# RWKV scans: the pairwise products of two heads on the two row halves of TensorE's array

## The chip, the core and the metric

The kernel runs on one of the eight cores of a Trainium2 chip. A core has five engines that run side by side, each with its own queue of instructions: TensorE (PE, matrix products; PEld are its weight loads), VectorE (DVE), ScalarE (ACT), GpSimd (POOL) and SyncE (SP, which here issues most DMAs). They work on SBUF, 128 partitions of on-chip memory; TensorE writes its results to PSUM, eight banks of 2 KB in each partition. A matmul multiplies a stationary operand (the weights, up to 128 rows by 128 columns) with a moving operand of up to 512 columns; the rows are what is summed over.

The metric is the time of one execution on the device in microseconds. The kernel before took 1816.26 us, the median of three runs (1816.13 to 1817.83).

## The reference

One layer of a hybrid encoder for 1024 tokens of width 1024, in float32: a normalized input is projected, the columns go to a windowed attention, to a bidirectional RWKV-7 mixer and to gates; an MLP with squared ReLU and a gated embedding follow. What the change touches is the RWKV mixer, a recurrence over the tokens, once forward and once backward, for 8 heads of 64:

```python
def rwkv7_bidir_scan(r, w, k, v, a, b):
    ...
    def step(state, inp):
        r_t, w_t, k_t, v_t, a_t, b_t = inp
        sa = jnp.einsum('dbhij,dbhj->dbhi', state, a_t)
        state = (state * w_t[..., None, :] + sa[..., :, None] * b_t[..., None, :]
                 + v_t[..., :, None] * k_t[..., None, :])
        y = jnp.einsum('dbhij,dbhj->dbhi', state, r_t)
        return state, y
```

## The kernel before

The recurrence is computed in chunks of 64 tokens: 16 chunks, two directions. The program takes them as 16 steps `s`; in each, direction `d=0` works on chunk `s` and `d=1` on chunk `15 - s`. Inside a chunk the recurrence becomes matrix products. For each head the scaled vectors of the chunk lie in DRAM as `ra_d` (the 64 columns of `a`, then the 64 of `r`) and `bk_d` (`b` and `k`), heads in four pairs: the 64 channels of a pair's even head on partitions 0 to 63, those of the odd head on partitions 64 to 127. `own` (line 692) names these halves.

**The products.** `products(s, d)` (line 1027) forms, for each head, all products of `b` and `k` with `a` and `r`: a block of 128 x 128 per head, summed over the 64 channels. A pair's two heads share the partitions, so before the change the moving operand `rms[d]` is a tile with two blocks of columns per pair: block 0 has the even head's rows, block 1 the odd head's, and the other rows are zeros, written once by two memsets on GpSimd (lines 790 to 792). One matmul of 128 rows by 256 columns then gives both heads. Two pairs fill one PSUM bank; VectorE multiplies the bank with a triangular mask and writes four heads of `gm`. Then `load_products` (line 795) asks SP for the operands of the next step.

**PSUM.** `ps_gps` (line 1024) takes a bank from a ring of two, tag `gps`. The ring is shared: the products (`gps`), the transposes of `operands` (`tmps`, line 1057), the blocks of `low_products` (`lps`, line 720), the quarter blocks of `inverse_off` (`qps`) and the sums of `epilogue` (`mups`). A bank can be written again when its reader is done.

**The rest of a step.** `wa_part` and `wb_part` sum `wps`; it is copied to `Wt` (lines 1086 and 1087), half on VectorE and half on ScalarE. `u_part` multiplies with the inverse `zi` into `ups`, copied to `UV` (lines 1095 and 1096). `s_part` (`sps`) makes the next state, `y_part` (`yps`) the output. Many of these are matmuls on 64 columns that alternate between the two column halves of the array. `load_step` (line 1040) loads the other operands, `operands` transposes `bkc` into `tm` and scales `rac`.

**The inverse.** Every four steps, `low_products` forms small blocks (`lps`, matmuls on quadrants of 64 x 64), `inverse` (line 734) inverts the 32 x 32 triangles of the next four steps on VectorE, with 62 elementwise instructions between transposes (`Lp`, `Z`, `Zn`, `Zt`), and `inverse_off` completes them on TensorE.

**The order.** Scan matmuls are issued through `mmo`, which keeps them in program order on TensorE. Between them `fill(n)` issues `n` matmuls of independent work (the generator `beside`: the gates' projection, `gmm`, then the attention's output, `uaps`), so that TensorE has something to do while other engines copy. The instructions of the other engines are put in order by the framework's scheduler before the kernel runs; each engine then works its queue in that order. A step `s` runs: products of step s+2, d=0; load_step; 5 fills; `lps` if s is 1, 5 or 9; 4 fills; `u_part`; 3 fills; products of step s+2, d=1; 4 fills; `lps` if s is 0, 4 or 8; `s_part`, `y_part`, `wa_part`; 5 fills; `operands`; 7 fills; at s = 3, 7, 11 the inverse's end; `wb_part`. Ahead of the loop stand the products of steps 0 and 1.

Of the kernel before, what the change touches and what calls it, by code (L numbers as in the profile page):

```python
# [9 lines left out]
F32 = mybir.dt.float32  # L10
F32R = mybir.dt.float32r
AF = mybir.ActivationFunctionType
ALU = mybir.AluOpType
# [4 lines left out]
P = 128  # L18
# [6 lines left out]
NP = 4  # L25
# [112 lines left out]
def block_kernel(ctx: ExitStack, tc: tile.TileContext, I: dict, out: bass.AP):  # L138
    nc = tc.nc

    def pool(stack, name, bufs=1, **kw):
        return stack.enter_context(tc.tile_pool(name=name, bufs=bufs, reuse_waits="tile", **kw))
# [4 lines left out]
    def const(name, shape):  # L147
        t_ = G.tile(shape, F32, name=name)
        nc.sync.dma_start(t_, I[name])
        return t_  # L150

    ra_d = DR.tile([ND, NCH, P, NP, P], F32, name="ra_d")
# [53 lines left out]
    def mmo(*a, **kw):  # L206

        tc.keep_in_program_order(nc.tensor.matmul(*a, **kw))  # L208
# [86 lines left out]
    with ExitStack() as s0:  # L295
# [98 lines left out]
        for t in range(NT):  # L394
# [8 lines left out]
            h, tq = divmod(t, 4)  # L403
            tsl = slice(tq * P, (tq + 1) * P)
            qkv = QW.tile([P, 768], F32, name="qkv", bufs=2)
            pss = [PT0.tile([P, 384], F32, name="psq", bufs=4) for _ in range(2)]
# [30 lines left out]
        for h in range(2):  # L437
            ps = PMM.tile([P, 512], F32, name="mm", tag="mm", bufs=2)
# [13 lines left out]
        for h in range(2):  # L452
            ps = PT0.tile([P, 512], F32, name="z13", tag="psq", bufs=4)
# [10 lines left out]
    gmask = const("gmask", [P, ND, P])  # L464
# [226 lines left out]
    NB = 4  # L691
    own = [slice(0, 64), slice(64, 128)]
    oth = [slice(64, 128), slice(0, 64)]

    def chunk(s, d):
        return s if d == 0 else NCH - 1 - s
# [90 lines left out]
    BP = pool(sB, "prod")  # L787
    zi = zi_tile(BI, "zi")

    rms = [BP.tile([P, 2, NP, P], F32, name=f"rm{i}") for i in range(2)]  # L790
    for t_ in rms:
        nc.gpsimd.memset(t_, 0.0)
    prods = {}

    def load_products(s, d):

        c = chunk(s, d)
        for q in range(2):
            nc.sync.dma_start(rms[d][own[q], q], ra_d[d, c][own[q]])
        b_ = BP.tile([P, NP, P], F32, name="bkp", bufs=2)  # L800
        nc.sync.dma_start(b_, bk_d[d, c])
        prods[s, d] = b_

    lts, zzs, lows = {}, {}, {}
    with ExitStack() as s2:
# [16 lines left out]
        for n in range(NT):  # L822
# [6 lines left out]
            for kv in range(2):  # L829
# [6 lines left out]
                for h in range(4):  # L836
                    sc = PA.tile([P, nk * P], F32, name="sc", tag="sc", bufs=2)
                    for j in range(2):
                        nc.tensor.matmul(sc, qT[:, 4 * kv + h, :], kT[:, kv, j, k0 * P:k1 * P], start=(j == 0), stop=(j == 1))
                    nc.vector.tensor_tensor_reduce(  # L840
                        out=sm[:, h, 0:nk * P], in0=sc, in1=band[:, b0:b0 + nk, :].rearrange("p b t -> p (b t)"), scale=1.0,
# [30 lines left out]
            if n == LOW_AT:  # L872
                lts[0] = list(low0)[-1]
                for d in range(ND):
                    load_products(0, d)
# [140 lines left out]
    gm = [AC[0].tile([P, NB, NH, P], F32, name=f"gm{d}", tag=f"ab{d}", bufs=1) for d in range(ND)]  # L1016
# [7 lines left out]
    def ps_gps(shape, name):  # L1024
        return PB.tile(shape, F32, name=name, tag="gps", bufs=2)

    def products(s, d):

        b_ = prods.pop((s, d))
        for h in range(2):  # L1030
            ps = ps_gps([P, 2, 2, P], "gps")
            for j in range(2):
                mmo(ps[:, j], b_[:, 2 * h + j, :], rms[d][:, :, 2 * h + j, :], start=True, stop=True)
            nc.vector.tensor_tensor(  # L1034
                out=gm[d][:, s % NB, 4 * h:4 * h + 4, :], in0=ps.rearrange("p j q t -> p (j q) t"),
                in1=gmask[:, d, :].unsqueeze(1).broadcast_to([P, 4, P]), op=ALU.mult)
        if s + 1 < NCH:
            load_products(s + 1, d)

# [106 lines left out]
    for d in range(ND):  # L1146
        products(0, d)
        fill(FILL0)
# [4 lines left out]
    def second_step():  # L1153
        fill(FILLQ)
        wps.append(wa_part(0))
        for d in range(ND):
            products(1, d)
            fill(FILL0)
# [5 lines left out]
    for s in range(NCH):  # L1164
# [21 lines left out]
        if more:  # L1186
            products(s + 2, 0)
# [150 lines left out]
    with ExitStack() as s7:  # L1338
# [16 lines left out]
        for i in (4, 5, 6, 7, 0, 1, 2, 3):  # L1355
            t = torder[i]
# [39 lines left out]
        for i in range(NT):  # L1396
# [6 lines left out]
            t = torder[i]  # L1403
# [282 lines left out]
    for ip, (lr_, rr_, bs, fresh) in enumerate(PRODS):  # L1686
        if fresh:
            banks[bs] = [acc() for _ in range(4)]
        for p in range(NPR):
# [5 lines left out]
            for i in range(4):  # L1695
                isl = slice(i * P, (i + 1) * P)
                for j, (x_, y_) in enumerate(((sh, th_), (sh, tl_), (sl, th_))):
                    nc.tensor.matmul(banks[bs][i], x_[:, isl], y_, start=fresh and p + j == 0,  # L1698
                                     stop=p == NPR - 1 and j == 2, skip_group_check=True)
# [8 lines left out]
            if ip == 0 and 0 <= p - (NPR - T1EARLY - NPRE) < NPRE:  # L1708
                q = p - (NPR - T1EARLY - NPRE)
# [3 lines left out]
            if ip == 1 and p % 2 == 0:  # L1713
                e, i = divmod(p // 2, 4)
                t = torder[4 * e + i]
# [11 lines left out]
        for i in range(4):  # L1727
            b_ = banks[bs][i]
# [87 lines left out]
```

## Time and profile before

| what | us |
|---|---|
| median of three runs | 1816.26 |
| profiled execution | 1818.63 |
| its span, first to last instruction | 1816.9 |
| the scan, from the first product to the last `yps` | 521.9 to about 884 |
| granted TensorE clock, mean over the span | 0.977 |

The profile is of one execution. A row of the timeline gives start, length, engine, line, operation, the tile written and the tiles read, and in brackets the idle time of the engine before it with what ended it. Matmuls are pipelined: the next one starts before the one before has ended, so lengths of single matmuls add up to more than the busy time, and the distance of starts is the rate. A float32 matmul leaves two records, one for each of its passes. `L208` is the helper `mmo`, so such rows are told apart by their tiles. A row of the view by stretches gives, for each engine, its busy time and its instructions in the stretch, then the granted clock.

### The profile page before, as it was taken

The numbers are of one execution on the slowest core, as the hardware profiler recorded it, in microseconds if no ns is written. First come the engines' busy times: TensorE is split into PE (matmuls) and PEld (weight loads), VectorE is DVE, ScalarE is ACT, GpSimd is POOL, SyncE is SP. The second block draws the span as 40 slices with busy tenths as digits, with TensorE's granted clock in tenths as the row PEclk, the third lists the DMA queues.
The fourth block names the chain that finished last, engine by engine and source line by source line (L and its number), as shares of the span: only waits on it lengthen the run. The fifth ranks groups of instructions, "written<-read, shape, count | busy, mean of one in ns | idle before, by whom it ended". The sixth has DMA issues, their size and how long they took to land. (4 is left out here: it accounts for less than half of the span.)

```text
span 1816.9 us, 29645 instructions
## 1 busy us (share of the span) xinstructions
PE 1714.2 (94%) x11288; PEld 1376.5 (76%) x11288; DVE 1135.8 (63%) x1931; ACT 883.1 (49%) x1624; POOL 321.7 (18%) x265
## 2 busy tenths in 40 slices
PE   7999888989999898988889989999999999999998
PEld 7977666766677777776667867888888888888887
DVE  5646777745845646575564277766766887685442
ACT  5546666547764555455542154544444444454221
POOL 3454544532132112112142000000000000000000
PEclk9999999999999999989999989999999999999999
DMA  5462344674377474576576214444456984574111
GB/s 198 99 183 81 117 145 145 197 202 115 98 201 203 141 196 148 158 199 197 175 225 198 93 47 151 151 152 161 143 163 214 324 262 122 187 221 135 62 41 47
DMA packets 281998, 285.96 MB, mean 157 GB/s; under 512 B 49408, under 2 KB 195712, under 8 KB 281728
## 3 DMA queue, kind: packets, MB, share of 16 engines
q1 hardware_dynamic: 273600, 270.76, 48.3%
q0 software_dynamic: 7824, 12.59, 2.5%
q8 instruction: 89, 1.46, 0.3%
q10 hardware_dynamic: 432, 0.73, 0.1%
q14 instruction: 53, 0.43, 0.1%
HBM read 203.26 MB, written 80.74 MB: 156 GB/s over the span
## 5 line engine op out<-in xcount | busy, mean ns | idle before, releaser
L188 POOL TENSOR_TENSOR wlo<-wst,whi 128x512 fp32r<-128x512 f32 x100 | 149.6, 1508 | 313.1 <-ACT whi L187 262.4
L1698 PE MATMUL ff2ps<-tl,sh 128*128 128x512 f32 x448 | 174.4, 389 | 0.1
L1698 PE MATMUL ff2ps<-th,sl 128*128 128x512 f32 x448 | 174.3, 389 | 0.0
L1698 PE MATMUL ff2ps<-th,sh 128*128 128x512 f32 x448 | 173.9, 389 | 0.0
L175 POOL TENSOR_TENSOR rstd<-ms,neghalf 128x1 f32<-128x1 f32 x24 | 13.3, 554 | 792.9 <-DVE ms L173 792.9
L187 ACT CAST sh<-sst 128x512 fp32r<-128x512 f32 x109 | 67.8, 622 | 99.5 <-PE ff2ps L1698 50.3
L188 DVE TENSOR_TENSOR sl<-sst,sh 128x512 fp32r<-128x512 f32 x109 | 75.1, 689 | 47.4 <-ACT sh L187 47.2
L1698 PEld LDWEIGHTS ff2ps<-tl,sh 128*128 128x128 f32 x448 | 84.1, 188 | 18.2 <-DVE tl L188 0.5
L1698 PEld LDWEIGHTS ff2ps<-th,sh 128*128 128x128 f32 x448 | 84.0, 188 | 17.7 <-ACT th L187 0.3
L1698 PEld LDWEIGHTS ff2ps<-th,sl 128*128 128x128 f32 x448 | 84.1, 188 | 17.5
L187 ACT CAST whi<-wst 128x512 fp32r<-128x512 f32 x100 | 60.7, 619 | 47.5 <-DMA wst<-in_w_in_dram 16.1
L187 ACT CAST w1h<-w1st 128x512 fp32r<-128x512 f32 x48 | 28.5, 621 | 101.1 <-DMA w1st<-in_w_ff_dram 64.1
L188 DVE TENSOR_TENSOR w1l<-w1st,w1h 128x512 fp32r<-128x512 f32 x48 | 31.9, 688 | 52.2 <-ACT w1h L187 52.2
L208 PE MATMUL gps<-rm,bkp 128*128 128x256 f32 x256 | 62.4, 386 | 1.3 <-ACT tm L1061 0.8
L1034 DVE TENSOR_TENSOR gm<-gps,gmask 128x512 f32<-128x512 f32 x64 | 43.7, 685 | 29.5 <-PE gps L208 29.5
L218 PE MATMUL gmm<-hh,wlo 128*128 128x512 f32 x144 | 59.3, 412 | 0.0
L214 PE MATMUL gmm<-hh,whi 128*128 128x512 f32 x144 | 59.2, 411 | 0.0
L216 PE MATMUL gmm<-hl,whi 128*128 128x512 f32 x144 | 59.2, 411 | 0.0
L1086 DVE COPY Wt<-wps 64x512 f32<-64x512 f32 x16 | 10.9, 680 | 71.3 <-PE wps L208 71.3
L208 PEld LDWEIGHTS gps<-rm,bkp 128*128 128x128 f32 x256 | 47.2, 189 | 10.9 <-issue 1.4
L226 PE MATMUL mm<-hh,whi 128*128 128x512 f32 x128 | 51.5, 402 | 3.3 <-ACT z L520 3.3
L188 DVE TENSOR_TENSOR w1l<-ssum,w1h 128x512 fp32r<-128x512 f32 x64 | 43.0, 688 | 16.9 <-ACT w1h L187 16.9
(409 smaller groups left out, 5056.8 us busy)
## 6 DMA issues: line engine op xcount, KB each, us to landing
wst<-in_w_in_dram SPq DMA_DIRECT2D x92, 256.0 KB, 3.5
tst<-in_w_ff_dram SPq DMA_DIRECT2D x80, 256.0 KB, 4.0
w1st<-in_w_ff_dram SPq DMA_DIRECT2D x32, 512.0 KB, 5.2
hid_S<-h SPq DMA_DIRECT2D x64, 256.0 KB, 2.1
sst<-hid_S SPq DMA_DIRECT2D x64, 256.0 KB, 2.8
hid_A<-h SPq DMA_DIRECT2D x48, 256.0 KB, 2.0
sst<-hid_A SPq DMA_DIRECT2D x45, 256.0 KB, 3.9
ra_d<-ra SPq DMA_DIRECT2D x8, 1024.0 KB, 4.5
```

The lines of the kernel that those rows point to most:

```text
L175: nc.gpsimd.tensor_tensor(out=r, in0=ms, in1=neghalf.broadcast_to([P, width]), op=ALU.pow)
L187: a = nc.scalar.copy(hi, src)
L188: b = (lo_eng or nc.vector).tensor_tensor(out=lo, in0=src, in1=hi.bitcast(F32), op=ALU.subtract)
L208: tc.keep_in_program_order(nc.tensor.matmul(*a, **kw))
L214: mm(ps, ah, bh, start=(i == 0), stop=False)
L216: mm(ps, ah, bl, start=False, stop=False)
L218: mm(ps, al, bh, start=False, stop=(i == n - 1))
L226: nc.tensor.matmul(ps, ah, bh, start=(i == 0), stop=False)
L1034: nc.vector.tensor_tensor(out=gm[d][:, s % NB, 4 * h:4 * h + 4, :], in0=ps.rearrange("p j q t -> p (j q) t"), in1=gmask[:, d, :].unsqueeze ...
L1086: nc.vector.tensor_copy(Wt[own[0], 0], wp[own[0]])
L1698: nc.tensor.matmul(banks[bs][i], x_[:, isl], y_, start=fresh and p + j == 0, stop=p == NPR - 1 and j == 2, skip_group_check=True)
```

## The change

The zeros go, and with them the memsets. `rms[d]` holds the pair's rows once, as they lie in DRAM, loaded by one DMA instead of two. Each pair's product becomes two matmuls of 64 rows by 128 columns: the even head on partitions 0 to 63, the odd head on 64 to 127, each with its own rows of the weights. All even heads of a direction go to one bank, all odd heads to the other; the mask is applied to each bank, and the four heads go to every second place of `gm`.

```diff
-    rms = [BP.tile([P, 2, NP, P], F32, name=f"rm{i}") for i in range(2)]
-    for t_ in rms:
-        nc.gpsimd.memset(t_, 0.0)
+    rms = [BP.tile([P, NP, P], F32, name=f"rm{i}") for i in range(2)]
     prods = {}
 
     def load_products(s, d):
 
         c = chunk(s, d)
-        for q in range(2):
-            nc.sync.dma_start(rms[d][own[q], q], ra_d[d, c][own[q]])
+        nc.sync.dma_start(rms[d], ra_d[d, c])
         b_ = BP.tile([P, NP, P], F32, name="bkp", bufs=2)
         nc.sync.dma_start(b_, bk_d[d, c])
         prods[s, d] = b_
...
     def products(s, d):
 
         b_ = prods.pop((s, d))
-        for h in range(2):
-            ps = ps_gps([P, 2, 2, P], "gps")
-            for j in range(2):
-                mmo(ps[:, j], b_[:, 2 * h + j, :], rms[d][:, :, 2 * h + j, :], start=True, stop=True)
+
+        pss = [ps_gps([P, NP, P], "gps") for _ in range(2)]
+        for j in range(NP):
+            for q in range(2):
+                mmo(pss[q][:, j], b_[own[q], j, :], rms[d][own[q], j, :], start=True, stop=True)
+        for q in range(2):
             nc.vector.tensor_tensor(
-                out=gm[d][:, s % NB, 4 * h:4 * h + 4, :], in0=ps.rearrange("p j q t -> p (j q) t"),
-                in1=gmask[:, d, :].unsqueeze(1).broadcast_to([P, 4, P]), op=ALU.mult)
+                out=gm[d][:, s % NB, q::2, :], in0=pss[q],
+                in1=gmask[:, d, :].unsqueeze(1).broadcast_to([P, NP, P]), op=ALU.mult)
         if s + 1 < NCH:
             load_products(s + 1, d)
```

## The prediction

> **What bounds the kernel now.** I read the page first: how busy each engine is over the whole span, and the row of the products that the change rewrites.
>
> ```profile
> span 1816.9 us, 29645 instructions
> PE 1714.2 (94%) x11288; PEld 1376.5 (76%) x11288; DVE 1135.8 (63%) x1931; ACT 883.1 (49%) x1624; POOL 321.7 (18%) x265
> ...
> L208 PE MATMUL gps<-rm,bkp 128*128 128x256 f32 x256 | 62.4, 386 | 1.3 <-ACT tm L1061 0.8
> ```
>
> TensorE (PE) is busy 94% of the span, and the 32 calls of `products` hold it for 62.4 us: 256 records, since each of the 128 float32 matmuls leaves two, one for each of its passes. So the first guess is that shorter products shorten the run. An average over stages can mislead, so I cut the scan into stretches and read each one.
>
> ```profile
> core 0: us, PE busy (x) PEld busy (x) DVE busy (x) ACT busy (x) POOL busy (x), PEclk, DMA share, GB/s
> 545.00:573.80 28.80, 28.31 (x390) 22.61 (x388) 8.88 (x13) 12.78 (x24) 4.46 (x5) 1.00 0.70 189
> 573.80:616.20 42.40, 36.06 (x460) 29.60 (x458) 40.39 (x83) 18.43 (x41) 10.14 (x11) 0.99 0.66 190
> ...
> 758.00:801.50 43.50, 36.16 (x528) 29.58 (x523) 42.02 (x101) 19.22 (x42) 7.36 (x9) 0.98 0.74 207
> 801.50:850.00 48.50, 45.55 (x648) 37.50 (x650) 22.24 (x33) 30.69 (x55) 8.96 (x8) 0.84 0.63 180
> ```
>
> The scan takes 16 steps, and every fourth one starts an `inverse` on VectorE (DVE). From 545.0 to 573.8 PE is busy 28.31 of 28.80 us and DVE 8.88: PE is the limit. From 573.8 to 616.2 it is turned round: DVE 40.39 of 42.40 us, PE 36.06. The view of waits says whether DVE waits for anything there, and the timeline how the stretch ends.
>
> ```profile
> DVE tmp L749 <- POOL Z L744: 0.2, 1, 0.2
> DVE gm L1034 <- PE gps L208: 0.2, 1, 0.2
> ```
>
> ```profile
> 613.76 1.85 DVE L756 STREAM_TRANSPOSE Zt<-Z 128x1024 f32<-128x1024 f32 x1
> 615.49 0.65 DVE L1095 COPY UV<-ups 64x512 f32<-64x512 f32 x1
> 616.07 1.25 DVE L1034 TENSOR_TENSOR gm<-gps,gmask 128x512 f32<-128x512 f32 x2
> ```
>
> ```profile
> 616.19 1.98 PE L208 MATMUL sps<-UV,tm 128*64 128x64 f32 x32 [4.04 <-DVE UV L1095]
> ```
>
> In 42.4 us DVE waits 0.4 us, and at the end PE stands still for 4.04 us until DVE, done with the inverse, copies `UV`. **Whatever PE saves inside such a stretch only lengthens that wait.** There are three (the third is 758.0 to 801.5: DVE 42.02 of 43.50 us), and in each lie five calls of `products`: d=1 of step 4k+1 and both of steps 4k+2 and 4k+3. That is 15 of the 32.
>
> **The change part by part.** *The matmuls.* A call now issues 4 matmuls of 128 rows by 256 columns, half of them zeros; then 8 of 64 rows by 128 columns, alternating between the array's two row halves. The trace has no 64x128 tile. Its nearest rows, first a stretch cut out around one burst of `lps` (length, then busy time and records of PE, PEld and ACT), then the timeline:
>
> ```profile
> 553.50:554.30 0.80, 0.69 (x32) 0.56 (x32) 0.00 (x0) 1.00 0.34 74
> ```
>
> ```profile
> 563.51 1.09 PE L208 MATMUL wps<-Sb,rac 128*64 128x128 f32 x16
> 564.54 1.99 PE L208 MATMUL gps<-rm,bkp 128*128 128x256 f32 x8
> ...
> 567.30 0.39 PE L208 MATMUL gmm<-hl,whi 128*128 128x512 f32 x1
> 567.62 0.27 PE L208 MATMUL lps<-la,lb 64*64 64x64 f32 x1
> ```
>
> ```profile
> 564.66 0.68 DVE L1086 COPY Wt<-wps 64x512 f32<-64x512 f32 x1 [6.93 <-PE wps L208]
> ```
>
> The first row is a burst of `lps`, quadrants of 64x64: 32 records in 0.69 us. They use both row halves, write two banks, and run on one another's heels, four abreast. The second is `wps`: 16 records that stream 128 columns, on alternating column halves, in 1.09 us, two abreast. The new product is also 16 records of 128 columns. A product now takes 1.99 us here and 1.89 on the step shown below, so a pass of 256 columns is (1.89 - 0.38)/7 = 0.216 us (0.38 being the own length of a record: the page's 386 ns) and one of 128 columns 0.108. If row halves overlap as column halves and quadrants do, its length is about that of `wps`, 1.09 us. If not, 16 passes of half the present length take what 8 whole ones do, 1.9 us. I take overlap, since `lps` shows both row halves at work at once.
>
> *The edges.* The array is now entered and left in another tile shape.
>
> ```profile
> 636.48 0.40 PE L208 MATMUL gmm<-hl,whi 128*128 128x512 f32 x1
> 636.81 1.15 PE L208 MATMUL ups<-Wt,zi 128*64 128x64 f32 x32
> 637.89 0.50 PE L208 MATMUL gmm<-hh,wlo 128*128 128x512 f32 x1
> 638.22 0.40 PE L208 MATMUL gmm<-hh,whi 128*128 128x512 f32 x1
> 638.46 0.40 PE L208 MATMUL gmm<-hl,whi 128*128 128x512 f32 x1
> 638.69 1.89 PE L208 MATMUL gps<-rm,bkp 128*128 128x256 f32 x8
> 640.23 0.58 PE L208 MATMUL gmm<-hh,wlo 128*128 128x512 f32 x1
> 640.65 0.39 PE L208 MATMUL gmm<-hh,whi 128*128 128x512 f32 x1
> ...
> 641.11 0.40 PE L208 MATMUL gmm<-hh,wlo 128*128 128x512 f32 x1
> 641.44 0.27 PE L208 MATMUL lps<-la,lb 64*64 64x64 f32 x1
> ```
>
> Into `ups`, a tiled shape, it takes 636.81 - 636.48 = 0.33 us; into `gps` of the full shape 638.69 - 638.46 = 0.23. The new shape costs 0.10 us more to enter. From the start of `ups` to the second `gmm` behind it are 638.22 - 636.81 = 1.41 us; `ups` streams 16 x 64 columns two abreast, the new product 8 x 128, as many. From the start of `gps` to the second `gmm` are 640.65 - 638.69 = 1.96 us. **A product behind `gmm` (d=1) gives back 1.96 - 1.41 - 0.10 = 0.45 us.** Behind `wps` (d=0) the array is in a tiled shape already and the product lasts 0.10 longer: 2.06 - 1.41 = **0.65 us**. All 32: 16 x 1.10 = 17.6 us.
>
> [...]
>
> *The evictions.* Both copies to `gm` now wait for all eight matmuls, since each bank gets its last block at the end, and both banks of the ring `gps` (two, shared with `lps`, `tmps`, `qps`) are held from the start. The order on DVE stays.
>
> ```profile
> 639.75 0.69 DVE L1034 TENSOR_TENSOR gm<-gps,gmask 128x512 f32<-128x512 f32 x1 [1.01 <-PE gps L208]
> 640.62 0.69 DVE L1034 TENSOR_TENSOR gm<-gps,gmask 128x512 f32<-128x512 f32 x1 [0.17 <-PE gps L208]
> ```
>
> ```profile
> 641.44 0.13 PEld L208 LDWEIGHTS lps<-la,lb 64*64 64x64 f32 x1 [0.37 <-DVE gm L1034]
> ```
>
> Now the copies end at 1.75 and 2.62 us after the product's start, and `lps`, 2.75 after it, goes 0.13 us behind the second. Then: the last pair starts at about 0.85 (seven waves of 0.108 and 0.1 for the edge). The second copy now starts 640.62 - (638.69 + 1.89 - 0.38) = 0.42 us behind the start of the last pass, 0.31 with a pass half as long: 1.16. Two copies back to back take 1.25 (the row at 616.07): 2.41; plus the 0.13, with rounding: **`lps` cannot start before 2.53 us, though PE would be there at 1.41 + 2 x 0.23 + 0.33 = 2.2**. So the d=1 product of steps 4k gives back only 2.75 - 2.53 - 0.10 = 0.12 us, and d=0 of steps 4k+1, which `lps` also follows (567.62 - 564.54 = 3.08), 3.08 - 2.53 = 0.55; `Wt` ahead of it on DVE ends at 565.34, before either copy. The strided target costs nothing by the equal count of elements; 0.1 us a copy would be 0.1 us at each such wait, 1 us in all.
>
> *The start.* Four calls, 521.9 to 541, each with four `gmm` and then the ring: 0.12 us apiece. Behind the first two PE stands still anyway:
>
> ```profile
> 535.85 0.63 PE L208 MATMUL wps<-UV,gm 128*64 128x64 f32 x14 [1.35 <-issue]
> ```
>
> I count two, 0.24 us. **Sum on PE:** start 0.24; steps 0 and 1, whose first product follows `gmm`, 0.45 + 0.12 + 0.55 = 1.12; steps 4, 5 and 8, 9, 2 x (0.65 + 0.12 + 0.55) = 2.64; steps 12 and 13, with no inverse and no `lps`, 2 x 1.10 = 2.20. Together **6.2 us** of the 17.6; bounds 0 and 17.6.
>
> *The memsets and the transfers.* `rms` loses its zeros, and with them two memsets.
>
> ```profile
> 375.47 1.86 POOL L792 MEMSET rm<- 128x1024 f32 x2
> 377.27 1.13 POOL L824 DMA_DIRECT2D qT<-qT_d  x2
> ```
>
> ```profile
> 384.06 0.71 PE L839 MATMUL sc<-kT,qT 128*128 128x256 f32 x4 [2.03 <-DMA qT<-qT_d]
> ```
>
> They stand ahead of the issue of `qT` on POOL, and PE then waits 2.03 us for `qT`. Without them the issue comes 1.86 us sooner. Bounds: 0, if the landing is set by the other transfers, and 1.86; I take **1.5 us**, near the upper, since the wait is longer than the memsets. On SP a load issues two DMAs for three, of the same bytes; SP is not what PE waits for in the stretches above, so nothing.
>
> *The clock.* The long wait at 616 has an aftermath.
>
> ```profile
> 616.19:618.86 2.67, 2.67 (x50) 2.67 (x52) 1.71 (x3) 2.60 (x3) 0.00 (x0) 0.50 0.00 0
> 618.86:622.00 3.14, 3.14 (x87) 2.98 (x84) 1.23 (x3) 1.34 (x4) 1.04 (x2) 1.00 0.41 121
> ```
>
> Behind the 4.04 us PE ran 2.67 us at half clock: 1.3 us lost on its path. From 801.5 to 850.0, behind the third inverse, the granted clock is 0.84: 0.16 x 48.5 = 7.8 us lost. The two calls of step 4k+3 lie before that wait and make it about 1.1 us longer, so I add **1.0 us** (bounds -1.3 and +5).
>
> Forecast: -6.2 - 1.5 + 1.0 = **-6.7 us**. The profiled execution, span and what lies around it, took 1818.63 us and would take 1811.9; it lay 2.4 above the median of the runs shown, 1816.26, so the median goes to **1809.6 us**.
>
> **The rivals.**
>
> *All of it counts* (17.6 + 1.9): 1797 us. It asks that DVE's order change so that `UV` no longer stands behind the inverse. For: PE's 94%. Against: the 4.04 us, and 0.4 us of DVE waits.
>
> *The clock takes it.* The gate closes behind more waits, or for longer: +5 in place of +1, 1813.6 us; with the memsets' 1.5 us hidden too, 1815. For: 0.84 behind the third inverse. Against: the stretch that PE fills, 545.0 to 573.8, has 1.00. [...]
>
> *The halves do not overlap*, the other side: row halves that stream 128 columns into all 128 partitions of two banks take turns. Then a product is 8 x 0.108 = 0.86 us longer than forecast: d=0 costs 0.21 more than now, d=1 0.41, and at the ring 0.31 and 0.74. Two calls at the start 1.5, steps 0 to 9 (0.41 + 0.74 + 0.31) + 2 x (0.21 + 0.74 + 0.31) = 4.0, the last two steps 1.2: +6.7, less 1.5, plus 1: 1822.5 us. It decides as soon as a pair's second half starts 0.1 us behind the first, instead of on its heels. Against it speaks `lps`. It is also the case where the change does not do what it says.
>
> **How the numbers follow.** Forecast 0.60 (its own range 1805 to 1812.5), clock 0.20, all of it 0.08, no overlap 0.07; 0.05 for an order of the engines that comes out otherwise, to either side. I leave out "all of it", "no overlap" and the tails: 1802 to 1817. About 0.2%, 3.6 us, is what a measurement of this kernel tells from no change: faster below 1812.6, slower above 1819.9. Faster: nearly all of the forecast, "all of it" and half of the rest, 0.68; same: the clock and the edge of the forecast, 0.22; slower: no overlap and the other tails, 0.10.
>
> **What would show it.** A burst of 16 `gps` records near 1.1 us, not 1.9. `lps` behind d=1 waiting for `gm` some 0.3 us. The wait of `sps` for `UV` near 616 longer than 4.04 us, the stretch still about 42 us. The wait for `qT` well under 2.03 us. Wrong I would be if DVE idled in that stretch, if the half-clock time beyond 600 us grew by more than 10 us, or if the ring held PE elsewhere too.

## The result and the profile after

The kernel after takes 1829.9 us, the median of nine runs (1821.07 to 1837.85), against 1818.22 for the kernel before (nine runs, 1816.13 to 1822.27): a ratio of 1.0053, with a 95% interval of 1.0035 to 1.0070. It is slower; the forecast was 1809.6 us. 0.001 of the ratio is 1.8 us here.

The profiled execution took 1830.82 us. From its page, the head and the costliest group of ACT, and then the view of the cores, first of after, then of before:

```profile
span 1829.0 us, 30110 instructions
PE 1714.9 (94%) x11544; PEld 1371.7 (75%) x11544; DVE 1137.5 (62%) x1931; ACT 883.1 (48%) x1624; POOL 317.5 (17%) x263
...
L1066 ACT ACTIVATE rac<-rac,Dt 128x128 f32<-128x128 f32 x120 | 39.2, 394 | 44.5 <-DMA rac<-ra_d 44.5
```

```profile
core 0: 1829.0 us, clock 0.968
```

```profile
core 0: 1816.9 us, clock 0.977
```

PE is busy as long as before (1714.2) although its work is shorter. An estimate from these rows: the clock missing from full speed was 0.023 x 1816.9 = 42 us and is 0.032 x 1829.0 = 59, so 17 us more were lost to half clock. PE's idle time was 1816.9 - 1714.2 = 102.7 and is 114.1, 11 us more. The span grew by 12, so the work itself, at full clock, fell by about 16 us. That is near the 17.6 counted for all 32 products. The saving was made, then given back twice: as waits and as half clock. (These are two single executions. Over all nine of after the mean clock is 0.970, over the 31 of before in the first comparison below 0.977: some 13 us.)

Which waits are new? The view of waits on PE, three rows of after:

```profile
PE tmps L1058 <- ACT lt L729: 7.1, 2, 3.7
PE qps L208 <- DVE Zn L755: 5.9, 1, 5.9
PE tmps L1058 <- ACT lv L983: 4.8, 1, 4.8
```

The first is not among before's at all; the other two were 4.5 and 2.5. Step 4 shows how the first arises. The timelines of PE and of ACT, after:

```profile
651.52 1.97 PE L1058 MATMUL tmps<-ident,bkc 128*128 128x128 f32 x8 [3.42 <-ACT lt L729]
```

```profile
650.81 0.40 ACT L1066 ACTIVATE rac<-rac,Dt 128x128 f32<-128x128 f32 x1 [6.08 <-DMA rac<-ra_d]
651.12 0.63 ACT L729 COPY lt<-lps 128x256 f32<-128x256 f32 x2
```

and ACT in the same step of before:

```profile
647.58 0.65 ACT L729 COPY lt<-lps 128x256 f32<-128x256 f32 x2 [1.81 <-PE lps L208]
651.39 0.69 ACT L1067 ACTIVATE rac<-rac,Dt 128x128 f32<-128x128 f32 x2 [3.16 <-DMA rac<-ra_d]
```

Line 1066 scales `rac`, an operand of step 6. In after its first piece stands **ahead** of the two `lt` copies in ACT's queue. ACT keeps to that order: it stands idle for 6.08 us until the transfer of `rac` lands, while the `lps` banks lie full behind it (the last of their matmuls started at 647.22 us, the first copy at 651.12); `tmps` needs one of these banks, and PE waits 3.42 us. In before the copies ran first, and the scaling waited behind them. Over the whole span ACT idles 44.5 us ahead of these scalings, in before 23.6. No line of the diff names `lt`, or the scaling. The order is the scheduler's, and it made another one for the changed program.

### The profile page after: what moved, and what is told of

It reads as the page before. It is cut to its first block, busy times and chain, and to the rows that moved or that the text cites. A ratio compares the mean times of both kernels' runs of the same rounds, so it can differ in the third digit from the quotient of the medians.

```text
span 1829.0 us, 30110 instructions
## 1 busy us (share of the span) xinstructions
PE 1714.9 (94%) x11544; PEld 1371.7 (75%) x11544; DVE 1137.5 (62%) x1931; ACT 883.1 (48%) x1624; POOL 317.5 (17%) x263
## 5 line engine op out<-in xcount | busy, mean ns | idle before, releaser
L1066 ACT ACTIVATE rac<-rac,Dt 128x128 f32<-128x128 f32 x120 | 39.2, 394 | 44.5 <-DMA rac<-ra_d 44.5
L752 DVE TENSOR_TENSOR Z<-Z,tmp 128x31 f32<-128x31 f32 (+15 forms) x124 | 50.2, 405 | 2.4
```

Of the source, the lines that this page charges most:

```text
L752: nc.vector.tensor_tensor(out=Z[:, t + 1:32, 0:m], in0=Z[:, t + 1:32, 0:m], in1=tv, op=ALU.add)
L1066: nc.scalar.activation(out=r_, in_=r_, func=AF.Copy, scale=Dt[:, d, j, s - 1:s])
```

## The experiments

`after(x, y)` is a helper of the kernel: it tells the scheduler to put x behind y on the same engine. Here it moves instructions of ACT; nothing computed changes. All kernels were timed in five rounds beside the kernel before, in four comparisons, each on another chip: e1 to e4, e5 to e8, e9 to e11, and e12 with e13. Where two experiments are compared, their ratios to before are subtracted and the half-widths of the intervals added as squares.

| kernel | median us | ratio to before, 95% interval |
|---|---|---|
| after | 1829.9 | 1.0053 (1.0035 to 1.0070) |
| e1 `lt` first | 1819.99 | 1.0010 (0.9994 to 1.0025) |
| e2 two loads | 1812.55 | 0.9971 (0.9952 to 0.9991) |
| e3 matmuls only | 1818.57 | 1.0002 (0.9984 to 1.0019) |
| e4 no overlap | 1827.99 | 1.0049 (1.0026 to 1.0072) |
| e5 after's order in before | 1820.20 | 1.0014 (0.9997 to 1.0031) |
| e6 `lt` and `pT` pins | 1828.18 | 1.0038 (1.0021 to 1.0056) |
| e7 two loads, `tm` first | 1802.92 | 0.9903 (0.9886 to 0.9921) |
| e8 one load, `tm` and `pT` pins | 1813.68 | 0.9971 (0.9955 to 0.9988) |
| e9 after, `tm` first | 1810.35 | 0.9958 (0.9942 to 0.9974) |
| e10 before, `tm` first | 1809.53 | 0.9959 (0.9944 to 0.9973) |
| e11 one load in the scan, `tm` first | 1805.20 | 0.9938 (0.9918 to 0.9958) |
| e12 e7 without overlap | 1803.51 | 0.9912 (0.9878 to 0.9947) |
| e13 matmuls only, `tm` first | 1802.93 | 0.9901 (0.9878 to 0.9924) |

**The order or the change itself?** e1 moves one scaling behind the `lt` copies, in after:

```diff
-                    nc.scalar.activation(out=r_, in_=r_, func=AF.Copy, scale=Dt[:, d, j, s - 1:s])
+                    a = nc.scalar.activation(out=r_, in_=r_, func=AF.Copy, scale=Dt[:, d, j, s - 1:s])
+                    if s in (6, 10):
+                        after(a, last_lt[-1])
```

> The changed kernel with one thing put back: at steps 4 and 8 ScalarE copies `lt` before it scales the `rac` of two steps later, which wait for their transfer. Theory A, order: the new order of the queues costs the time, and of its 12.1 us (profiled span 1829.0 against 1816.9) this place costs about 3.5 us at each of two steps, wait and clock; so 1821 to 1824 us, and the waits of tmps for lt (3.7 us at 740, 3.4 at 648) are gone. Theory B, the products themselves (both banks held, eviction late, the clock closing behind longer waits): within 2 us of the changed kernel, 1828 to 1832.

e2 takes back the single load and keeps the rest:

```diff
-        nc.sync.dma_start(rms[d], ra_d[d, c])
+        for q in range(2):
+            nc.sync.dma_start(rms[d][own[q]], ra_d[d, c][own[q]])
```

> The changed kernel with the operand still loaded by two DMAs of one half each, as before; everything else as changed. In its ScalarE queue `lt` stands ahead of `rac` again at steps 4 and 8. Theory A: the order came from the DMA that is saved, so 1810 to 1819 us, with the product's gain showing. Theory B: 1826 to 1832, as the same matmuls, banks and evictions run.

e3 puts only the new matmuls and banks into before, with the zeros, the memsets and the two loads:

```diff
-                mmo(ps[:, j], b_[:, 2 * h + j, :], rms[d][:, :, 2 * h + j, :], start=True, stop=True)
+                mmo(pss[q][:, j], b_[own[q], j, :], rms[d][own[q], q, j, :], start=True, stop=True)
```

> The kernel before with the new matmuls and banks alone: the zeros, the memsets and the two loads stay. Its ScalarE queue also has `lt` first. Theory A: 1811 to 1818 us (the forecast's 6.2 us of TensorE time less 1 for the clock, without the 1.5 us of the memsets; somewhat more if the queues come out otherwise). Theory B: 1825 or more.

e4 is after with neighbouring matmuls on the same rows:

```diff
-        for j in range(NP):
-            for q in range(2):
+        for q in range(2):
+            for j in range(NP):
```

> The changed kernel with the eight matmuls in the other order: the four even heads first, then the four odd heads, so that neighbours use the same rows and cannot overlap. A burst of the products should last about 16 x 0.108 + 0.27 = 2.0 us against 1.17. Its ScalarE queue has `lt` first at steps 4 and 8. If the overlap is worth on the path what the forecast said, it lies 8 to 13 us above the variant with two loads; if TensorE's time in the products does not matter at all, within 3 us of it.

e1 and e3 came out some 1 us outside their ranges, e2 inside its own, and e4 15 us above e2, where 8 to 13 were expected. e1 wins back 0.43% of after's time with no other difference than ACT's order (and a few issues on SP and POOL); the `tmps` waits for `lt` are gone from its trace. e2 wins back 0.82% (half-width 0.27) and is faster than before. So neither the matmuls nor the banks made after slow. e3 shows that this is not the whole story: without the new load and without losing the memsets, the new matmuls alone gain nothing. e4 is level with after and 0.78% (half-width 0.30) behind e2. That looked like the price of the overlap; but e4 has one load and another order than both (its ACT runs the `lt` copies first, as before did), so it was taken up again in e12, at one order.

**How much of it is the order?** Four more, in one comparison. e5 gives before the order of after at the one place, e6 adds to e1 a pin in the attention part, where `po` of after waits for a `pT` copy behind a weight cast:

```profile
395.94 0.62 ACT L187 CAST whi<-wst 128x512 fp32r<-128x512 f32 x1 [2.77 <-DMA wst<-in_w_in_dram]
396.47 0.37 ACT L861 COPY pT<-pt 128x256 f32<-128x256 f32 x1
```

```diff
# e5, in before; a is the scaling of step 6 or 10
+                        for l in last_lt[-6:-4]:
+                            after(l, a)
# e6, in after, beside the pin of e1
+            if len(casts) in behind:
+                after(casts[-1], copies[behind[len(casts)] - 1])
```

> The kernel before, with one thing moved: on ACT the first scaling of rac of steps 6 and 10 stands ahead of the second pair of lt copies, as in the kernel after. Products, zero tile, memsets and both half loads are those of before; PE, DVE and POOL have the order of before, SP issues seven transfers in another order. Theory A (the order on ACT costs the time): pinning it back gave after 9.9 us (1829.9 to 1820.0), so here it costs 7 to 11 us: 1825 to 1828 us against 1817.4, with PE waits tmps <- ACT lt of some 3.4 us in steps 4 and 8 and half clock behind each. Theory B (the order matters only together with the new products or the single load): 1817.4 within 2 us.

> The kernel after, one load, with two orders on ACT put back: lt copies ahead of the first scaling of rac (as in e1_lt_first, 1820.0), and one weight cast (whi) of the attention part behind the pT copy that it held up. Theory A: the PE wait po <- pT of 3.58 us at 390.84 and the half clock behind it go, the scan's first product starts some 6 us earlier than in e1_lt_first (519 to 521 for 525.63), and the time is 1813 to 1815 us, that of e2_two_loads (1812.6). Theory B (one transfer of 128 rows is itself slower to serve than two of 64): the scan starts late in any order, 1820 within 2 us.

e7 and e8 use a wider pin: the scalings of a step behind the `tm` copies of the step before it. e7 is e2 with it, e8 is after with it and with the pin of the cast.

```diff
-            nc.scalar.copy(t_, tp.rearrange("p q (h j) -> p (q h) j", h=2))
+            tms[s] = nc.scalar.copy(t_, tp.rearrange("p q (h j) -> p (q h) j", h=2))
...
+                    if s - 1 in tms:
+                        after(a, tms[s - 1])
```

> e2_two_loads (1812.6) with both tm copies of a step ahead of all scalings of rac of the next step on ACT; PE and DVE keep the order of e2_two_loads but for two rows. Theory A (what costs is a copy that PE needs behind an ACT operation that waits for its transfer): the PE waits lps <- tm of 2.53 us at 731.48 and tmps <- lv of 3.93 us at 820.20 shrink to under 1.5 us, with less half clock: 1805 to 1810 us. Rival: those waits are covered by DVE anyway, or the later rac holds up wps: 1811 to 1815 us.

> The kernel after, one load, with tm copies ahead of the next step's scalings of rac, and the weight cast behind the pT copy as in e6_both_pins. Theory A: the same waits go as in e7_two_tm and e6_both_pins together: 1805 to 1811 us, faster than before by some 0.5%. Theory B (the single load costs by itself): 1813 us or more, by the 7 us that part e1_lt_first from e2_two_loads.

Only e7 went as theory A said, 2 us beyond its range. e5 was to cost 7 to 11 us and cost 0.14%, 2.5 us, with an interval from -0.5 to 5.6. The waits came as expected (`tmps` for `lt`, 6.3 us in two). But before waits there too, one instruction group later, for a `tm` copy that stands behind the same scaling, and this wait is gone in e5: the one replaces the other. The row of before:

```profile
652.61 0.27 PE L208 MATMUL lps<-la,lb 64*64 64x64 f32 x1 [2.34 <-ACT tm L1061]
```

So the one place does not explain after. e6 was to reach 1814 us and fell back to 1828. The wait of the attention part did not go: a cast that waits for its transfer still stands in front of a `pT` copy:

```profile
396.69 0.62 ACT L187 CAST whi<-wst 128x512 fp32r<-128x512 f32 x1 [3.75 <-DMA wst<-in_w_in_dram]
397.21 0.36 ACT L868 COPY pT<-pt 128x256 f32<-128x256 f32 x1
```

The order of PE changed with it, and the scan's first product came at 532.0 us, for 525.6 in e1. e7 took 1802.9 us. Its trace no longer has the `tmps` wait for `lv`, which stands in after at step 13 with the same pattern, a scaling that waits 4.15 us for its transfer in front of what PE needs:

```profile
839.54 0.69 ACT L1066 ACTIVATE rac<-rac,Dt 128x128 f32<-128x128 f32 x2 [4.15 <-DMA rac<-ra_d]
840.26 1.28 ACT L983 ACT_TABLE_LOAD   x1
841.55 0.69 ACT L983 ACTIVATE lv<-mups,gne 128x512 f32<-128x512 f32 x1
842.14 0.62 ACT L989 ACTIVATE ysq<-y 128x512 f32<-128x512 f32 x1
842.66 0.58 ACT L1060 COPY tm<-tmps 128x512 f32<-128x512 f32 x1
```

e8 was to reach 1805 to 1811 us, or 1813 and more if the single load costs by itself. It took 1813.7, so it went against the order as the only cause; e11 below takes up the load. The pin of the cast does not help: e9, which has the `tm` pin without it, lies at 0.9958 for 0.9971 (half-width of the difference 0.23%).

**The pin alone, in both kernels.** e9 is after and e10 is before, each with the `tm` pin and nothing else: on PE not one instruction changes its place, on DVE two rows do. e11 is e7 with one load from step 1 on.

> The kernel after, one load, with nothing changed but that both tm copies of a step stand ahead of all scalings of rac of the next step on ACT (PE keeps the order of after in full, DVE but for two rows). Theory A (ACT copies that PE needs stand behind a scaling that waits for its transfer): the tmps waits of 3.42 and 3.72 us in steps 4 and 8 and the 4.77 us in step 13 go or shrink, with the half clock behind them; by e1_lt_first (9.9 us) and e7_two_tm (9.6 us) together 1812 to 1818 us against 1829.9 for after. Rival (these waits are an effect of running at a lower clock, or are taken over by other waits): 1824 us or more.

> The kernel before with the same one pin: both tm copies of a step ahead of all scalings of rac of the next step on ACT. Old products, zero tile, memsets, two loads; PE, POOL and SP keep the order of before in full, DVE but for two rows. It parts the pin from the products in e7_two_tm (1802.9, ratio 0.9903). If the products are worth what the forecast's sum says (6.2 us, with the memsets 7.7), this gives 1809 to 1813 us, ratio some 0.995 to 0.9975; if the products are worth nothing and the order is all, 1803 us, ratio 0.990; if the pin does nothing for the old products, 1817.8.

> e7_two_tm with the two half loads kept for step 0 alone (they are issued in the attention part) and one load of 128 rows in the 15 later steps. Theory A (one load costs only through the order that the attention part comes out in): the scan's first product starts at 519 to 521 us as in e7_two_tm and the time is 1802 to 1807 us. Theory B (each single load costs by itself): 15 steps lose it, 1809 us or more although the scan starts early.

This is the answer to the slower time. (e10 and e11 lie inside their ranges, e9 2 us below its own.) The pin alone takes 0.95% (half-width 0.24), 17 us, from after; it takes 0.41% from before. **With it, after and before are equal: 0.9958 and 0.9959.** ACT's idle time ahead of the scalings, from the groups of e9 and then of e10:

```profile
  DMA rac<-ra_d: 12.9, 10
```

```profile
  DMA rac<-ra_d: 7.5, 7
```

The `tmps` waits for `lt` are gone from e9's trace. And the stretch from the `sps` behind the first inverse to the start of the second (length, then busy time and instructions of PE, PEld, DVE, ACT and POOL, granted clock, DMA), in after, then before, then e9:

```profile
615.29:666.57 51.28, 47.18 (x880) 38.53 (x880) 12.08 (x19) 28.61 (x59) 8.26 (x10) 0.90 0.55 153
```

```profile
616.19:666.10 49.91, 47.19 (x848) 39.18 (x848) 13.33 (x21) 28.91 (x59) 8.11 (x9) 0.94 0.55 152
```

```profile
613.31:658.45 45.14, 44.82 (x880) 37.03 (x880) 12.11 (x19) 28.48 (x59) 8.25 (x10) 0.95 0.57 164
```

The same 880 matmul records take 51.28 us in after and 45.14 in e9, where PE is idle for 0.32 us in place of 4.10.

e11 lies between e9 and e7. Of the 0.55% (half-width 0.24) that e7 is ahead of e9, one load in the scan has 0.35 (0.27), so some of it; the rest, 0.20 (0.26), is not resolved. The profiles show where: the scan's first product starts at 525.0 us in e9, at 521.4 in e11 and at 519.9 in e7, and `qps` waits 6.0, 5.9 and 4.8 us for `Zn`. Between e9 and e11 the order of the attention part differs. Between e11 and e7 PE has one order, and ACT differs in some scalings and casts; whether that or the larger transfer itself costs the time no run shows.

**Is it the products, and their overlap?** e7 is 0.56% (0.23) ahead of e10, but the two differ in products, tile, memsets and order. e12 takes the overlap out of e7 by the edit of e4, e13 is e3 with the `tm` pin.

> e7_two_tm (1802.9, ratio 0.9903) with the new products issued one half of the array's rows after the other (all four of q = 0, then all four of q = 1), so that neighbouring matmuls share their rows; PE keeps the order of e7_two_tm but for that, DVE differs in 96 rows. If the overlap of the row halves is what the products gain on the path: a burst takes about 1.9 us for 1.17, and 17 of 32 stand on the path, so 6 to 13 us are lost: 1809 to 1816 us, ratio 0.9935 to 0.9975. Rival (the products are covered everywhere, and e7's gain is order and memsets): 1803 us within 2, ratio 0.990.

> e10_before_tm_first (1809.5, ratio 0.9959) with the new matmuls and banks alone: operand tile with zeros, both memsets and both half loads stay as before, tm copies ahead of the scalings of rac. If the products' term of the forecast holds (6.2 us on the path) this gives 1802 to 1805 us, ratio 0.991 to 0.993. Rival (the gain of e7 over e10 comes from memsets and tile, or from the order in the attention part): 1807 to 1811 us, ratio 0.995 to 0.997.

e13: the matmuls and banks alone, with zeros, memsets and two loads as before, are 0.58% (0.27) ahead of e10, 10 us. Tile and memsets add nothing that can be seen. Unpinned (e3) the same matmuls gained nothing: in its trace `lps` and `qps` wait 5.9 us for `tm` (3.6 in before), and the mean clock of its twelve executions is 0.973 for 0.977 of before, 7 us.

e12 missed: no loss can be measured, +0.09% (0.39) against e7; the 6 to 13 us expected are 0.33 to 0.71%, and the interval leaves the lower part of that open. The overlap is real, as the rows of one product in e7 and in e12 show:

```profile
545.47 1.16 PE L208 MATMUL gps<-rm,bkp 64*128 64x128 f32 x16
546.56 0.50 PE L208 MATMUL gmm<-hh,wlo 128*128 128x512 f32 x1
```

```profile
546.70 1.71 PE L208 MATMUL gps<-rm,bkp 64*128 64x128 f32 x16
548.34 0.50 PE L208 MATMUL gmm<-hh,wlo 128*128 128x512 f32 x1
```

Start to next start is 1.09 us with and 1.64 without it (1.54 in before, 640.23 - 638.69): 0.55 us a product, 17.6 for all. Of these, 15 x 0.55 = 8 us belong to the 15 products that lie under DVE's inverse. There a shorter product only brings PE earlier to `ups`, which needs DVE's copy `Wt`. The view of waits on PE, e7, then e12:

```profile
PE ups L208 <- DVE Wt L1090: 6.2, 5, 2.4
```

```profile
PE ups L208 <- DVE Wt L1090: 0.8, 3, 0.4
```

So 5.4 of the 8 us are waits in e7. And the granted clock of e12's profile is 0.982, e7's 0.978:

```profile
core 0: 1801.5 us, clock 0.982
```

```profile
core 0: 1802.8 us, clock 0.978
```

By the same estimate as above, 0.004 x 1802 = 7 us less half clock; the means over all executions, 0.981 of six and 0.9785 of four, make it 5. One stretch of e7 shows the two together: behind the longest of its waits for `Wt`, 2.43 us up to 769.09, PE ran at half clock for 3.41 us.

```profile
769.53:772.94 3.41, 3.18 (x33) 2.62 (x33) 3.41 (x9) 0.80 (x2) 0.00 (x0) 0.50 1.00 276
```

The covered 8 us and the clock are 13 to 15 of the 17.6. With so few executions, and an interval this wide, it is a reading, not a proof. What stays open with it: why the matmuls gain 10 us (e13), when e12, whose products last no shorter than before's, is still 0.47% (0.37) ahead of e10. Some 6 us of that are clock (mean 0.981 for 0.978). In the traces of e10 and e13 PE has one order apart from the products, DVE and ACT do not, so part of the 10 us may be a luckier order. No run parted the two.

The best version is e7: the change with its two half loads kept and the `tm` copies ahead of the next scalings, 0.9903 (0.9886 to 0.9921).

## Why the prediction was wrong

**The failed step** is that the change was taken to leave the queues as they were: "The order on DVE stays", and of the load that is saved, "SP is not what PE waits for in the stretches above, so nothing". The sum was made on before's queues with shorter products in them, and a change of order got 0.05, "to either side". But the queues are written by a scheduler from the whole program, and every engine came out in another order. The order on ACT alone is worth 17 us in after (e9 against after), three times the 6.2 us of the sum. Before had the same weakness for 7 us (e10), to be read in its own trace: ACT idle for 3.16 us at 651.39 in front of a scaling, with `tm` and PE's `lps` behind it. The one load, put at nothing, costs 0.82% (e2 against after), and with the pin still 0.55% (e7 against e9). From the measured +0.53% to the -0.56% of e7 against e10 are 1.09%: half is what the pin is worth more in after than in before (0.95 less 0.41), half the load.

**The clock** was mis-sized: forecast 1.0 us (bounds -1.3 and 5, the 5 a guess that no row gives), measured about 17 between the two profiles, 13 over all executions. What the prediction named as refuting it, half clock beyond 600 us grown by over 10 us, came: from 600 to 1100 us the mean clock fell from the first row (before) to the second (after), 0.02 of 500 us by these rounded figures. Read in ten stretches of 50 us, the lost clock is 23.5 us before and 37 after, so some 27 us more ran at half.

```profile
600.00:1100.00 500.00, 449.04 (x4706) 359.39 (x4705) 296.05 (x499) 233.70 (x431) 91.03 (x82) 0.95 0.53 158
```

```profile
600.00:1100.00 500.00, 440.62 (x4841) 349.82 (x4840) 285.03 (x485) 228.71 (x423) 91.71 (x82) 0.93 0.51 158
```

That is what the rival "the clock takes it" names, more half clock, but with the new waits: in e9, which has the shorter products without these waits, the clock from 600 to 1100 us is 0.95 again.

**What held.** The product, after:

```profile
637.54 0.40 PE L208 MATMUL gmm<-hl,whi 128*128 128x512 f32 x1
637.86 1.16 PE L208 MATMUL gps<-rm,bkp 64*128 64x128 f32 x16
638.96 0.50 PE L208 MATMUL gmm<-hh,wlo 128*128 128x512 f32 x1
639.29 0.39 PE L208 MATMUL gmm<-hh,whi 128*128 128x512 f32 x1
...
640.08 0.33 PE L208 MATMUL lps<-la,lb 64*64 64x64 f32 x2
640.40 0.27 PE L208 MATMUL lps<-lb,la 64*64 64x64 f32 x1
```

A burst of 16 records in 1.16 us (forecast 1.09); entry 637.86 - 637.54 = 0.32 (0.33); start to the second `gmm` 1.43 for 1.96, so 0.53 less, and with the 0.09 us more of entry (0.32 for 0.23) 0.44 given back where 0.45 was forecast. `lps` for the second bank goes 2.54 us after the start (2.53), for the first one already at 2.22. A copy to the strided `gm` takes 0.68 us (0.69 before). The halves overlap, so the rival on the slower side was not the reason for the slower time.

Of the stretches that DVE bounds, the first two kept their length:

```profile
573.50:614.70 41.20, 35.48 (x490) 28.50 (x488) 39.46 (x82) 18.49 (x41) 10.00 (x10) 0.96 0.66 194
666.57:707.60 41.03, 34.23 (x490) 27.45 (x488) 39.29 (x82) 18.41 (x41) 10.06 (x10) 1.00 0.62 190
758.65:809.70 51.05, 40.91 (x675) 34.09 (x675) 48.85 (x103) 22.85 (x48) 9.49 (x10) 0.91 0.71 206
```

Here each row runs from the start of `Lp` to the end of `Zt`. Measured so, before had 41.8, 41.9 and 47.1 us. The third grew, and the end of its chain, `qps` on `Zn`, came late with it. The wait of `sps` for `UV` was to grow beyond 4.04 us and was 3.96: what PE saves shows earlier in these stretches, as `ups` waiting for `Wt`, 4.3 us in after for 1.0 in before. That the saving is covered there held, the place of the wait did not.

The wait for `qT` was to shrink by 1.5 us from 2.03 and shrank to 0.92:

```profile
381.97 0.71 PE L836 MATMUL sc<-kT,qT 128*128 128x256 f32 x4 [0.92 <-DMA qT<-qT_d]
```

But the scan's first product starts at 526.0 us, 4.1 later than before: other waits of the attention part have eaten this gain and more: 2.6 us for `pT` (1.6 before), 3.3 for `smk` (1.8), and 1.8 for a `wlo` that before does not wait for.

**The sum itself** is not confirmed. With the change as made, one load, and the same pin on both sides, the gain is nothing (0.9958 and 0.9959, half-width of the difference 0.22%). Its 7.7 us before the clock, 0.42%, are met only with the two loads kept: 0.56% (0.23; e7 against e10). And that fit may be luck: e13, which keeps the memsets that the sum counts at 1.5 us, gains as much, and e12, with products no shorter than before's, nearly as much.

## What to carry to other kernels

Where a scheduler writes the queues, a change to the number or length of any instruction can rewrite the order of all engines; compare the order in the two traces before explaining a time, and look in the trace of before for work that waits on a transfer in front of a copy that TensorE needs: such a place is a gain to be had (17 us in after, 7 in before), and a risk in every other change. Pin those few places first, then judge a change with the same pins on both sides. Price a wait of TensorE by what follows it too: here 2.67 us at half clock behind one of 4.04 us in before, some 16 behind one of 5.90 in after.

## What was unexpected of the hardware

Half clock also followed a short wait. In after PE had no new matmul for 1.81 us up to 522.46 (the first row covers it); from 523.69 a stretch of 3.41 us ran at 0.50, then the clock was full again:

```profile
520.60:522.50 1.90, 0.09 (x2) 0.04 (x1) 0.00 (x0) 0.00 (x0) 1.72 (x2) 1.00 0.72 202
523.69:527.10 3.41, 3.41 (x16) 2.43 (x16) 0.00 (x0) 1.76 (x4) 1.88 (x2) 0.50 0.88 266
527.10:530.00 2.90, 2.90 (x30) 2.30 (x28) 1.29 (x2) 2.34 (x8) 0.67 (x1) 1.00 0.81 246
```

PE was busy for the whole of that half-clocked stretch. The wait ahead of it was less than half as long as the 4.04 us in before, which had 2.67 us of half clock behind them and a mean clock of 0.69 in their last 1.19. And behind the 5.90 us of `qps` in after the clock stayed at half for far longer, with PE busy throughout (0.53 over these 17.1 us are some 16 at half):

```profile
808.00:825.10 17.10, 17.05 (x304) 14.76 (x305) 4.40 (x7) 11.63 (x20) 1.29 (x1) 0.53 0.41 122
```

Behind 5.99 us in e9 it was 10.2 us, the last 2.3 of the wait among them. What sets this length the runs do not show.
